# Seven block products in place of eight for the down and gate projections of a two-layer decoder trunk

## The chip, the cores and the metric

The kernel runs on one core of a Trainium2 chip. The metric is the time of one execution in device microseconds (us); each kernel is run several times and the median is given. TensorE is called PE, VectorE DVE, ScalarE ACT, GpSimd POOL, and the queue that issues most loads SP.

## What is computed

Two layers, 512 tokens, model width 1024, hidden width 4096, all in float32. Each layer is a token mixer (an mLSTM in the first, sliding-window attention in the second), and behind it come the parts that the change touches: a squared-ReLU MLP with a residual and a layer norm, and a gated per-layer input.

```python
x = layer_norm(ALPHA * x + mix, mix_ln_g[i], mix_ln_b[i])
x = layer_norm(ALPHA * x + square(relu(x @ w_up[i])) @ w_down[i], mlp_ln_g[i], mlp_ln_b[i])
x = x + sigmoid(x @ w_gate[i] + b_gate[i]) * (p[i] @ w_proj[i])
```

`w_up` is 1024x4096, `w_down` 4096x1024, `w_gate` 1024x1024, `w_proj` 256x1024.

## The kernel before

Each float32 matrix product is made of three PE matmuls (`mm3`, lines 87 to 90): every operand is split into a high part in the format fp32r and a low part that is what remains, and high*high, high*low and low*high are summed in PSUM. A split is a copy on ACT (line 76) and a subtraction on DVE, for some weights on POOL (line 77). Weights stream from memory in tiles of 128x1024 (`load_w`): the raw tile `wraw` has 3 buffers, the parts `whi` and `wlo` have 6 each, so the split for a tile waits until the tile six places before it has been used by PE.

The residual stream lives in four tiles `res` of 128 tokens x 1024. `XH` and `XL` hold the two parts of x, transposed (contraction on partitions), for all 512 tokens.

- `mlp` takes the hidden width in two halves of 2048 columns. For each, 16 up products (`wstat`, one weight tile each, 24 matmuls of 512 tokens) are squared by ACT and DVE and split into `hh` and `hl`. Then down: for each half of the 1024 output columns, four PSUM banks (one for 128 tokens each) collect 16 contraction blocks, 16*3 matmuls of 512 columns to a bank; `add_res` adds the bank to `res`. Behind the last one `ln_finish` normalises a tile of tokens and `transpose_in` puts it into `XH` and `XL`.
- `ple` takes the two halves of the output columns: for each 128 tokens first the `w_proj` product (2*3 matmuls), then the gate product (8*3 matmuls); DVE adds the bias, ACT takes the sigmoid, DVE multiplies and adds to `res`. In layer 0 it then transposes x for the next layer, scales `res` on POOL and spills it.

In what follows a line number is that of the kernel of which it is told; the changed kernel has its own. The order on each engine is set by a scheduler that the framework runs over the program, within the dependences; on the chip each engine and each DMA queue works through its own list in that order. PSUM has 5 banks for products (`mm`) and 3 for transposes (`tp`).

## Time and profile before

| what | value |
| --- | --- |
| median of 3 runs | 1259.3 us (1258.25 to 1262.23) |
| span of the profiled execution | 1256.3 us |
| median less span (what lies around the span) | 3.0 us |
| mean granted PE clock | 0.994 |
| busy PE / DVE / ACT / POOL | 1225.7 / 645.7 / 439.6 / 181.7 us |

The profile gives one execution, and for it no time but the span, so 3.0 us is the median's distance from it. A group line of the profile gives line, engine, operation, output <- inputs, shapes and count, then busy time and mean duration in ns, then the idle time of the engine just before these instructions and who ended it. A timeline line gives start and duration in us and, in brackets, the idle time before it. Durations of instructions that follow each other overlap by some tens of ns, matmuls by more, so the time that one costs is read from start to start.

### The profile page before, as it was taken

Reading aid. Unit: us, or ns where it says so; the run is one execution under the profiler, and the core shown is the slowest. Engines: PE = TensorE matmul, PEld = TensorE weight load, DVE = VectorE, ACT = ScalarE, POOL = GpSimd, SP = SyncE. Lnnn points to the kernel's source line nnn. Section 1 sums busy time; section 2 is a strip of 40 time slices with the busy share of each in tenths; the row PEclk is TensorE's granted clock in tenths of the full one; section 3 lists DMA queues with packets and bytes.
Section 4 is the critical chain, followed back from the end, with each engine's and each line's share of the span. In section 5 each row is a group of like instructions: output and inputs, shape, how many; then the busy total and the mean of one; then the engine's idle time right before and its main releaser. Section 6 shows DMA issues by size and latency. Waiting matters only on the chain.

```text
span 1256.3 us, 15515 instructions
## 1 busy us (share of the span) xinstructions
PE 1225.7 (98%) x6110; PEld 1041.3 (83%) x6110; DVE 645.7 (51%) x1061; ACT 439.6 (35%) x766; POOL 181.7 (14%) x261
## 2 busy tenths in 40 slices
PE   8999999999999999999999899999999999999998
PEld 8899987888888888888889788788888888888887
DVE  7556565744323444238555778485433244423663
ACT  4544542443212343123334555234322134421230
POOL 1011113200000000003076553530000000000100
PEclk9999999999999999999999999999999999999999
DMA  7222225333222423124233111443323332322231
GB/s 245 89 88 68 84 68 201 118 118 101 83 86 72 133 97 101 68 95 140 93 118 117 52 34 35 150 136 101 101 68 96 105 113 90 101 86 82 74 119 42
DMA packets 35704, 124.53 MB, mean 99 GB/s; under 512 B 4064, under 2 KB 4592, under 8 KB 35632
## 3 DMA queue, kind: packets, MB, share of 16 engines
q1 hardware_dynamic: 33552, 116.46, 28.1%
q0 software_dynamic: 2080, 7.09, 1.6%
q8 instruction: 48, 0.79, 0.2%
q14 instruction: 24, 0.20, 0.0%
HBM read 119.34 MB, written 4.19 MB: 98 GB/s over the span
## 4 chain that ended last, share of the span: by engine, by line
PE 86%; DVE 6%; DMA 3%; ACT 2%; issue 2%; POOL 1%; SPq 0%; ACTq 0%; DVEq 0%; POOLq 0%
PE mm L88 27%; PE mm L90 27%; PE mm L89 27%; PE tp L129 1%; DMA res<-in_x_dram 1%; DMA xraw<-in_xT_dram 1%; ACT pr L693 1%; DVE res L146 1%; DMA res<-spill 1%; PE tp L88 1%; PE tp L89 1%; PE tp L90 1%; DVE QS L662 1%; POOL rs L138 0%; DVE pr L697 0%
## 5 line engine op out<-in xcount | busy, mean ns | idle before, releaser
L76 ACT CAST whi<-wraw 128x1024 fp32r<-128x1024 f32 (+1 forms) x200 | 207.6, 1039 | 554.0 <-PE mm L90 291.2
L77 DVE TENSOR_TENSOR wlo<-wraw,whi 128x1024 fp32r<-128x1024 f32 (+1 forms) x176 | 214.7, 1223 | 357.7 <-ACT whi L76 356.8
L89 PE MATMUL mm<-XL,whi 128*128 128x512 f32 (+1 forms) x640 | 235.4, 369 | 0.0
L90 PE MATMUL mm<-XH,wlo 128*128 128x512 f32 (+1 forms) x640 | 235.3, 369 | 0.0
L88 PE MATMUL mm<-XH,whi 128*128 128x512 f32 (+1 forms) x640 | 234.3, 369 | 0.7 <-ACT ot L225 0.7
L88 PE MATMUL mm<-whi,hh 128*128 128x512 f32 x512 | 202.7, 396 | 0.0
L89 PE MATMUL mm<-wlo,hh 128*128 128x512 f32 x512 | 202.6, 396 | 0.0
L90 PE MATMUL mm<-whi,hl 128*128 128x512 f32 x512 | 202.5, 395 | 0.0
L88 PE MATMUL mm<-whi,XH 128*128 128x512 f32 (+2 forms) x424 | 146.7, 346 | 0.9 <-DVE s L554 0.5
L90 PE MATMUL mm<-whi,XL 128*128 128x512 f32 (+2 forms) x424 | 147.1, 347 | 0.0
L89 PE MATMUL mm<-wlo,XH 128*128 128x512 f32 (+2 forms) x424 | 146.5, 346 | 0.0
L88 PEld LDWEIGHTS mm<-XH,whi 128*128 128x128 f32 x640 | 120.1, 189 | 21.1 <-ACT ot L225 1.2
L90 PEld LDWEIGHTS mm<-XH,wlo 128*128 128x128 f32 x640 | 120.9, 189 | 19.9
L89 PEld LDWEIGHTS mm<-XL,whi 128*128 128x128 f32 x640 | 120.9, 189 | 19.8
L138 POOL TENSOR_TENSOR rs<-rs,nhalf 128x1 f32<-128x1 f32 x16 | 22.8, 1426 | 732.1 <-DVE rs L137 732.1
L90 PEld LDWEIGHTS mm<-whi,hl 128*128 128x128 f32 x512 | 96.5, 188 | 23.0
L88 PEld LDWEIGHTS mm<-whi,hh 128*128 128x128 f32 x512 | 96.5, 188 | 22.9
L89 PEld LDWEIGHTS mm<-wlo,hh 128*128 128x128 f32 x512 | 96.5, 188 | 22.8
L89 PEld LDWEIGHTS mm<-wlo,XH 128*128 128x128 f32 x424 | 81.7, 193 | 8.2 <-issue 1.5
L88 PEld LDWEIGHTS mm<-whi,XH 128*128 128x128 f32 x424 | 81.4, 192 | 8.0 <-DVE q L652 0.8
L90 PEld LDWEIGHTS mm<-whi,XL 128*128 128x128 f32 x424 | 81.5, 192 | 6.5 <-issue 0.8
L77 POOL TENSOR_TENSOR wlo<-wraw,whi 128x1024 fp32r<-128x1024 f32 x24 | 58.9, 2463 | 55.0 <-ACT whi L76 55.0
(246 smaller groups left out, 1476.8 us busy)
## 6 DMA issues: line engine op xcount, KB each, us to landing
wraw<-in_w_up_dram SPq DMA_DIRECT2D x64, 512.0 KB, 3.6
wraw<-in_w_down_dram SPq DMA_DIRECT2D x64, 512.0 KB, 3.5
wraw<-in_w_gate_dram SPq DMA_DIRECT2D x16, 512.0 KB, 3.5
wraw<-in_w_vo_dram SPq DMA_DIRECT2D x19, 412.0 KB, 3.2
wraw<-in_w_qk_dram SPq DMA_DIRECT2D x8, 512.0 KB, 4.5
wraw<-in_w_out_dram SPq DMA_DIRECT2D x8, 512.0 KB, 3.9
wraw<-in_w_q_dram SPq DMA_DIRECT2D x8, 512.0 KB, 3.4
wraw<-in_w_o_dram SPq DMA_DIRECT2D x8, 512.0 KB, 3.4
```

The source lines that it names most:

```text
L76: ACT.copy(hi, raw)
L77: eng.tensor_sub(lo, raw, f32(hi))
L88: PE.matmul(o, lh, rh, start=start, stop=False)
L89: PE.matmul(o, lh, rl, start=False, stop=False)
L90: PE.matmul(o, ll, rh, start=False, stop=stop)
L129: PE.transpose(pt[:, tsl(j)], src[:, tsl(b + j)], ident)
L138: GP.tensor_tensor(dst, dst, nhalf[:, :n], ALU.pow)
L146: V.scalar_tensor_tensor(res[t], res[t], rs, b, ALU.mult, ALU.add)
L662: V.tensor_sub(QS[other, hs, tsl(t)], pv[own], f32(QS)[own, hs, tsl(t)])
L693: ACT.activation(pt_[:, par, pr, :], scs[pr][:, par, :], AF.Exp, scale=ASCALE, bias=nm[:, par, pr:pr + 1], accum_out=sm[:, par, pr:pr + 1])
```

## The change

A product of two matrices in 2x2 blocks takes eight block products; the change takes seven, with sums of blocks on both sides (Winograd's form of Strassen's scheme). It is used for down and for the gate. The blocks of the activations are A11, A12 (tokens 0 to 255), A21, A22 (tokens 256 to 511), split over the contraction; those of the weights are r11, r21 (output columns 0 to 511) and r12, r22 (columns 512 to 1023). The products, in this order, with the operand on the left that is named in the code: M1 = A11 r11, M2 = A12 r21, M5 = S1 (r12-r11), M6 = S2 (r22-r12+r11), M7 = S3 (r22-r12), M3 = S4 r22, M4 = A22 (r22-r12+r11-r21). Here S1 = A21+A22, S2 = S1-A11, S3 = A11-A21, S4 = A12-S2.

- `mlp` now takes the hidden width in four quarters of 1024 columns: 8 up products, then `seven`, in which each product takes 128 tokens (a = 0, then 1) x 512 columns x 4 contraction blocks: 2*4*3 = 24 matmuls of 512 columns, two PSUM banks.
- The sums of activations are made in `evac` of the last four up products of a quarter, on POOL (four subtractions or additions of 128x256 for each), and split by ACT and DVE (`both_parts`). Tiles `S23` hold S2 and S3, `S4A` holds S4 and A22.
- The sums of weights are eight POOL subtractions of 128x1024 in each `seven`, written over the raw tiles; each result is split again, so a `seven` has 14 splits of 128x1024 where these products had 8.
- The results are summed by `on`: DVE adds banks to `res` and to a tile `T`, POOL adds `T` to `res`.
- The square now is one DVE instruction that reads the PSUM bank (line 605) and a copy of the relu by ACT; before it was two ACT instructions and a DVE product in SBUF (lines 485 to 487).
- The layer norm in front of the gate writes its sums of blocks by `put_seven` (copies by ACT, sums by DVE and POOL, seven splits for two tiles of tokens); the layer norm in front of the MLP scales `res` by ALPHA on POOL, which `add_res` did before.
- `ple` makes all eight `w_proj` products first and copies them to SBUF; `p` lies in a part of `XH`, `XL` that the gate no longer reads. The gate's `on` has DVE and POOL steps like that of `mlp`.
- The raw weights of `seven` lie in six buffers `rb` and two of `wraw`; broadcast biases have 2 buffers where there were 4.

The core of the diff (`ple` has the same pattern with its own `on`):

```diff
-    def ln_finish(t, st, g, b, xh=True):
+    def ln_finish(t, st, g, b, put=None):
         mv = small.tile([P, 2], F32, tag="mv", name="mv")
         V.bn_aggr(mv, st)
         rs = small.tile([P, 1], F32, tag="rs", name="rs")
         rsqrt_eps(rs, mv[:, 1:2], 1)
         V.scalar_tensor_tensor(res[t], res[t], mv[:, 0:1], g, ALU.subtract, ALU.mult)
         V.scalar_tensor_tensor(res[t], res[t], rs, b, ALU.mult, ALU.add)
-        transpose_in(res[t], t, XH, XL)
+        if put is None:
+            transpose_in(res[t], t, XH, XL)
+            GP.tensor_scalar(res[t], res[t], ALPHA, 0.0, ALU.mult, ALU.add)
+        else:
+            put(t)
...
+    def seven(A_, wsrc, on):
+
+        w0, w1 = wsrc(0), wsrc(1)
+        r11, r21 = two((w0, 0, True)), two((w0, 2, False))
+        r12, r22 = two((w1, 0, True)), two((w1, 2, True))
+
+        def ops(raw):
+            out = []
+            for c in range(2):
+                hi = wpool.tile([P, 1024], F32R, tag="whi", name="whi", bufs=6)
+                lo = wpool.tile([P, 1024], F32R, tag="wlo", name="wlo", bufs=6)
+                split(raw[c], 1024, hi, lo)
+                out.append((hi, lo))
+            return out
+
+        def product(name, w, step):
+            banks = [mm_bank(), mm_bank()]
+            for a in range(2):
+                for k in range(4):
+                    h, l = A_[name](k, a)
+                    wh, wl = w[k // 2]
+                    sl = slice((k % 2) * 512, (k % 2 + 1) * 512)
+                    mm3(banks[a], h, l, wh[:, sl], wl[:, sl], k == 0, k == 3)
+                on(step, a, banks[a])
+
+        product("A11", ops(r11), "M1")
+        product("A12", ops(r21), "M2")
+        for c in range(2):
+            GP.tensor_sub(r11[c], r12[c], r11[c])
+        product("S1", ops(r11), "M5")
+        for c in range(2):
+            GP.tensor_sub(r12[c], r22[c], r12[c])
+            GP.tensor_sub(r11[c], r22[c], r11[c])
+        product("S2", ops(r11), "M6")
+        product("S3", ops(r12), "M7")
+        product("S4", ops(r22), "M3")
+        for c in range(2):
+            GP.tensor_sub(r21[c], r11[c], r21[c])
+        product("A22", ops(r21), "M4")
...
+    def both_parts(dst, src, eng=V):
+
+        ACT.copy(dst[0], src)
+        eng.tensor_sub(dst[1], src, f32(dst[0]))
...
+    def put_seven(t):
+
+        a = t % 2
+        raws = []
+        for b in range(2):
+            pt = tp_bank()
+            for j in range(4):
+                PE.transpose(pt[:, tsl(j)], res[t][:, tsl(4 * b + j)], ident)
+            raw = xr()
+            ACT.copy(raw, pt)
+            raws.append(raw)
+            if t < 2:
+                v = raw.rearrange("p (k c) -> p k c", c=P)
+                both_parts((XH[:, 4 * b:4 * b + 4, tsl(t)], XL[:, 4 * b:4 * b + 4, tsl(t)]), v)
+        if t < 2:
+            half0[t] = raws
+            return
+        a11, a12 = half0[a]
+        a21, a22 = raws
+        s1 = xr()
+        V.tensor_add(s1, a21, a22)
+        GP.tensor_sub(a21, a11, a21)
+        V.tensor_sub(a11, s1, a11)
+        V.tensor_sub(a12, a12, a11)
+        sl = tsl(a)
+        kc = lambda x: x.rearrange("p (k c) -> p k c", c=P)
+        both_parts([x[:, :, sl] for x in sp["S1"]], kc(s1))
+        both_parts([x[:, 0, :, sl] for x in sp["S23"]], kc(a11))
+        both_parts([x[:, 1, :, sl] for x in sp["S23"]], kc(a21))
+        both_parts([x[:, 0, :, sl] for x in sp["S4A"]], kc(a12))
+        both_parts([x[:, 1, :, sl] for x in sp["S4A"]], kc(a22))
...
             def evac(ps, j, a, b):
-                r = pm.tile([P, S], F32, tag="relu", name="relu", bufs=3)
-                ACT.activation(r[:, a:b], ps[:, a:b], AF.Relu)
-                ACT.activation(hh[j // 2][:, j % 2, a:b], r[:, a:b], AF.Square)
-                V.tensor_mul(r[:, a:b], r[:, a:b], r[:, a:b])
-                V.tensor_sub(hl[j // 2][:, j % 2, a:b], r[:, a:b], f32(hh[j // 2])[:, j % 2, a:b])
-            nj = 2 * NPAIR
+                if j >= 4 or a == 0:
+                    h = xr()
+                    if j < 4:
+                        h0[j] = h
+                else:
+                    h = h0[j]
+                ACT.activation(h[:, a:b], ps[:, a:b], AF.Relu)
+                V.scalar_tensor_tensor(h[:, a:b], ps[:, a:b], 0.0, h[:, a:b], ALU.max, ALU.mult)
+                k = j % 4
+                if j < 4:
+                    if a == 0:
+                        both_parts([x[:, k, :] for x in A11], h[:, :256])
+                    return
+                g = h0[k]
+                both_parts([x[:, k, :] for x in A12], h[:, :256])
+                s1 = pm.tile([P, 256], F32, tag="s1", name="s1", bufs=2)
+                GP.tensor_add(s1, g[:, 256:], h[:, 256:])
+                GP.tensor_sub(g[:, 256:], g[:, :256], g[:, 256:])
+                GP.tensor_sub(g[:, :256], s1, g[:, :256])
+                GP.tensor_sub(h[:, :256], h[:, :256], g[:, :256])
+                both_parts([x[:, k, :] for x in sp["S1"]], s1)
+                two_ = lambda x: x.rearrange("p (b c) -> p b c", c=256)
+                both_parts([x[:, :, k, :] for x in sp["S23"]], two_(g))
+                both_parts([x[:, :, k, :] for x in sp["S4A"]], two_(h))
...
+                lo_, hi_ = slice(0, 512), slice(512, 1024)
+                r0, r1 = res[a], res[2 + a]
+                if step == "M1":
+                    ACT.copy(T[:, a, :], bank)
+                    GP.tensor_add(r0[:, lo_], r0[:, lo_], T[:, a, :])
+                elif step == "M2":
+                    V.tensor_add(r0[:, lo_], r0[:, lo_], bank)
+                    if last:
+                        V.bn_stats(sts[a][:, 0, :], r0[:, lo_])
+                elif step == "M5":
+                    V.tensor_add(r1[:, hi_], r1[:, hi_], bank)
+                    V.tensor_add(r0[:, hi_], r0[:, hi_], bank)
+                elif step == "M6":
+                    V.tensor_add(T[:, a, :], T[:, a, :], bank)
+                    GP.tensor_add(r0[:, hi_], r0[:, hi_], T[:, a, :])
+                elif step == "M7":
+                    V.tensor_add(T[:, a, :], T[:, a, :], bank)
+                    GP.tensor_add(r1[:, hi_], r1[:, hi_], T[:, a, :])
+                    GP.tensor_add(r1[:, lo_], r1[:, lo_], T[:, a, :])
+                    if last:
+                        V.bn_stats(sts[2 + a][:, 1, :], r1[:, hi_])
+                elif step == "M3":
+                    V.tensor_add(r0[:, hi_], r0[:, hi_], bank)
+                    if last:
+                        V.bn_stats(sts[a][:, 1, :], r0[:, hi_])
+                        ln_finish(a, sts[a], g_, b_, put_seven)
+                elif step == "M4":
+                    V.tensor_sub(r1[:, lo_], r1[:, lo_], bank)
+                    if last:
+                        V.bn_stats(sts[2 + a][:, 0, :], r1[:, lo_])
+                        ln_finish(2 + a, sts[2 + a], g_, b_, put_seven)
+
+            at = lambda pair: lambda k, a: tuple(p[:, k, tsl(a)] for p in pair)
+            seven(sset((at(A11), at(A12))), lambda half: [A["w_down"][i, half, 4 * q + c] for c in range(4)], on)
```

Three places of the order. The first is POOL's list in a quarter. Before, from the last layer norm ahead of the MLP of layer 0 to the first ones behind it, this is all that POOL has:

```order
L138 TENSOR_TENSOR rs_2090<-rs_2090,nhalf_71 128x1
L121 DMA bc_4578<-in_ple_b_gate_dram 128x1024
L121 DMA bc_4580<-in_b_b_o_dram 128x1024
L138 TENSOR_TENSOR rs_4351<-rs_4351,nhalf_71 128x1
L138 TENSOR_TENSOR rs_4398<-rs_4398,nhalf_71 128x1
L138 TENSOR_TENSOR rs_4445<-rs_4445,nhalf_71 128x1
```

After, this stands there in the third quarter of layer 0, from the first sum for the third contraction block to the sum that S2 of the last one needs (`rb` and `wraw` are raw weights, `xr` the activations, `s1` is S1); right ahead of it stands the first of the line 520 subtractions:

```order
L614 TENSOR_TENSOR s1_3763<-xr_3592,xr_3758 128x256
L525 TENSOR_TENSOR wraw_3825<-rb_3821,wraw_3825 128x1024
L615 TENSOR_TENSOR xr_3592<-xr_3592 128x256
L520 TENSOR_TENSOR rb_3823<-rb_3835,rb_3823 128x1024
L614 TENSOR_TENSOR s1_3810<-xr_3628,xr_3805 128x256
L616 TENSOR_TENSOR xr_3592<-s1_3763,xr_3592 128x256
L646 TENSOR_TENSOR res0_1745<-res0_1745,T_2129 128x512
L525 TENSOR_TENSOR wraw_3827<-rb_3823,wraw_3827 128x1024
L646 TENSOR_TENSOR res1_1746<-res1_1746,T_2129 128x512
L615 TENSOR_TENSOR xr_3628<-xr_3628 128x256
L617 TENSOR_TENSOR xr_3758<-xr_3758,xr_3592 128x256
L616 TENSOR_TENSOR xr_3628<-s1_3810,xr_3628 128x256
```

Between the sums of activations (lines 614 to 617) stand subtractions of weights (lines 520 and 525) and two additions to `res` (line 646), which wait for M1.

The second is DVE's list at the same place, the end of the up products and the first block products. Before, in the first half of the MLP of layer 0, behind the last up product:

```order
L77 TENSOR_TENSOR wlo_2969<-wraw_2967,whi_2968 128x1024
L77 TENSOR_TENSOR wlo_2975<-wraw_2973,whi_2974 128x1024
L77 TENSOR_TENSOR wlo_3085<-wraw_3083,whi_3084 128x1024
L77 TENSOR_TENSOR wlo_3091<-wraw_3089,whi_3090 128x1024
L154 SCALAR_TENSOR_TENSOR res0_1745<-res0_1745,mm_2831 128x512
L154 SCALAR_TENSOR_TENSOR res1_1746<-res1_1746,mm_2832 128x512
L154 SCALAR_TENSOR_TENSOR res2_1747<-res2_1747,mm_2833 128x512
L77 TENSOR_TENSOR wlo_3097<-wraw_3095,whi_3096 128x1024
L77 TENSOR_TENSOR wlo_3103<-wraw_3101,whi_3102 128x1024
```

After, in the third quarter (line 77 splits weights, line 543 activations, lines 648 to 653 add banks to `res`):

```order
L77 TENSOR_TENSOR wlo_3956<-rb_3821,whi_3955 128x1024
L77 TENSOR_TENSOR wlo_3960<-rb_3823,whi_3959 128x1024
L543 TENSOR_TENSOR S1l_2124<-s1_3810,S1h_2123 128x256
L543 TENSOR_TENSOR S23l_2126<-xr_3592,S23h_2125 128x2x256
L648 TENSOR_TENSOR res0_1745<-res0_1745,mm_3883 128x512
L77 TENSOR_TENSOR wlo_3994<-rb_3829,whi_3993 128x1024
L77 TENSOR_TENSOR wlo_3998<-rb_3831,whi_3997 128x1024
L648 TENSOR_TENSOR res1_1746<-res1_1746,mm_3884 128x512
L652 TENSOR_TENSOR res2_1747<-res2_1747,mm_3921 128x512
L653 TENSOR_TENSOR res0_1745<-res0_1745,mm_3921 128x512
L543 TENSOR_TENSOR S4Al_2128<-xr_3758,S4Ah_2127 128x2x256
L543 TENSOR_TENSOR S23l_2126<-xr_3628,S23h_2125 128x2x256
```

The last row is the low part of S2 and S3 of the last contraction block, which M6 reads; ahead of it stand four splits of weights, for M6 and M7, and the additions for M2 and M5.

The third is DVE's list where the MLP of layer 0 ends and the gate begins. Before (layer norm of the second tile of tokens, up to the splits of the first for `XL`):

```order
L152 TENSOR_TENSOR res1_1746<-res1_1746,mm_4176 128x512
L519 BN_STATS lst_2120<-res1_1746 128x6
L142 BN_AGGR mv_4396<-lst_2120 128x2
L137 TENSOR_SCALAR rs_4398<-mv_4396 128x1
L145 SCALAR_TENSOR_TENSOR res1_1746<-res1_1746,mv_4396,bc_3919 128x1024
L146 SCALAR_TENSOR_TENSOR res1_1746<-res1_1746,rs_4398,bc_3921 128x1024
L134 TENSOR_TENSOR XL_65<-tp_4356,XH_64 128x4x128
L134 TENSOR_TENSOR XL_65<-tp_4363,XH_64 128x4x128
```

After, at the layer norm's end (lines 145 and 146 are the layer norm's two large steps):

```order
L145 SCALAR_TENSOR_TENSOR res2_1747<-res2_1747,mv_4777,bc_4443 128x1024
L146 SCALAR_TENSOR_TENSOR res1_1746<-res1_1746,rs_4728,bc_4445 128x1024
L77 TENSOR_TENSOR wlo_5060<-rb_4959,whi_5059 128x1024
L137 TENSOR_SCALAR rs_4779<-mv_4777 128x1
L145 SCALAR_TENSOR_TENSOR res3_1748<-res3_1748,mv_4827,bc_4443 128x1024
L137 TENSOR_SCALAR rs_4829<-mv_4827 128x1
L77 TENSOR_TENSOR wlo_5064<-rb_4961,whi_5063 128x1024
L146 SCALAR_TENSOR_TENSOR res2_1747<-res2_1747,rs_4779,bc_4445 128x1024
L543 TENSOR_TENSOR XL_65<-xr_4699,XH_64 128x4x128
L543 TENSOR_TENSOR XL_65<-xr_4708,XH_64 128x4x128
L146 SCALAR_TENSOR_TENSOR res3_1748<-res3_1748,rs_4829,bc_4445 128x1024
L543 TENSOR_TENSOR XL_65<-xr_4738,XH_64 128x4x128
```

The rows of `XL` for the first tokens, which M1 of the gate reads, now stand behind the layer norm of the third tile of tokens and behind weight splits for M5 (`wlo` from `rb`).

More of the change, by code (lines that the diff above doesn't have):

```diff
@@ L541, in ple @@
                 for k in range(2):
+                    j = k * NT + t
+                    h, l = (x[:, j // 2, (j % 2) * P:(j % 2 + 1) * P] for x in spare)
                     sl = slice(k * 512, (k + 1) * 512)
[L543 to L559 removed]
@@ L560, in ple @@
-                if last:
-                    continue
-                if half == 1:
-                    transpose_in(res[t], t, XH, XL)
-                    GP.tensor_scalar(res[t], res[t], ALPHA, 0.0, ALU.mult, ALU.add)
-                    GP.tensor_add(res[t], res[t], bo)
-                    nc.sync.dma_start(spill[t], res[t])
+                    mm3(pj, h, l, wph[:, sl], wpl[:, sl], k == 0, k == 1)
+                pjs[t, half] = pp.tile([P, 512], F32, name=f"pj{t}{half}")
+                ACT.copy(pjs[t, half], pj)
@@ new lines, in ple, with done @@
+        if not last:
+            bo = bcast(A["b_b_o"])
+        def done(t):
+            if last:
+                return
+            transpose_in(res[t], t, XH, XL)
+            GP.tensor_scalar(res[t], res[t], ALPHA, 0.0, ALU.mult, ALU.add)
+            GP.tensor_add(res[t], res[t], bo)
+            nc.sync.dma_start(spill[t], res[t])
+        at = lambda b: lambda k, a: tuple(p[:, 4 * b + k, tsl(a)] for p in (XH, XL))
+        seven(sset((at(0), at(1))), lambda half: [A["w_gate"][i, half, c] for c in range(4)], on)
@@ L783, in yoco_kernel @@
     psum_pools(pctx, mm=5, tp=3)
+    c7 = seven_pools(1, "left")
     mlp(1, "left")
     ple(1, True, "left")
+    c7.close()
     pctx.close()
```

144 lines of the change are left out of this document (90 added, 54 removed).

## The prediction

> **What bounds the kernel now.** I read the page first, then the chain that ended last, then the MLP stage by stage, then single instructions of DVE and POOL where both were at work. The page and the chain:
>
> ```profile
> span 1256.3 us, 15515 instructions
> PE 1225.7 (98%) x6110; PEld 1041.3 (83%) x6110; DVE 645.7 (51%) x1061; ACT 439.6 (35%) x766; POOL 181.7 (14%) x261
> ...
> PE 86%; DVE 6%; DMA 3%; ACT 2%; issue 2%; POOL 1%; SPq 0%; ACTq 0%; DVEq 0%; POOLq 0%
> ```
>
> PE is the bound, and POOL is nearly idle. Two stages of the first MLP, an up and a down half (start and end, length, busy time of PE, PEld, DVE, ACT, POOL, granted clock, DMA share, GB/s):
>
> ```profile
> 231.00:318.00 87.00, 87.00 (x472) 75.64 (x471) 44.60 (x62) 35.08 (x55) 2.55 (x3) 1.00 0.35 111
> 318.00:405.00 87.00, 87.00 (x373) 69.97 (x372) 21.98 (x22) 15.49 (x16) 0.00 (x0) 1.00 0.24 80
> ```
>
> PE waits for nothing there, and POOL does nothing in the down half. What a matmul costs is read from starts: the down matmuls of each half (first and last start in the row), the first up matmul behind them, and 24 gate matmuls:
>
> ```profile
> L88 PE MATMUL mm<-whi,hh x128: 392/397/400, 318.4 to 407.6; 128*128 128x512 f32 x128
> ...
> 408.34 0.39 PE L88 MATMUL mm<-XH,whi 128*128 128x512 f32 x1
> ...
> L88 PE MATMUL mm<-whi,hh x128: 390/397/477, 495.4 to 586.4; 128*128 128x512 f32 x128
> ...
> 1237.86 0.39 PE L88 MATMUL mm<-whi,XH 128*128 128x512 f32 x1
> ...
> 1243.08 0.40 PE L90 MATMUL mm<-whi,XL 128*128 128x512 f32 x1
> ```
>
> Down: 408.34-318.4 = 89.9 us for 384, 0.234 each. Up: 495.4-408.34 = 87.1 for 384, 0.227. Gate: 5.22 us for 23 steps, 0.227.
>
> **What is removed.** A down quarter had 192 matmuls of 512 columns and has 7*24 = 168; there are 8 quarters: 192 fewer, 192*0.234 = 44.9 us. Each gate has 168 where 192 stood: 48*0.227 = 10.9. Together **-55.8 us**, if PE never waits. The weights are loaded once as before. On SP the raw tiles of a quarter, six of which wait for DVE's splits, now stand ahead of all but the first of the next up tiles;
>
> ```profile
> wraw<-in_w_up_dram SPq DMA_DIRECT2D x64, 512.0 KB, 3.6
> ```
>
> an up tile lands in 3.6 us and is used for 5.4, with DMA engines busy for 0.24 to 0.35: nothing, or 3.6 us a quarter if the first came late. ACT gets 6 more splits a quarter and about as many copies as it loses; with 35 us busy in 87 it has room: nothing.
>
> **What is added, and what covers it.** The rows that price it:
>
> ```profile
> L77 POOL TENSOR_TENSOR wlo<-wraw,whi 128x1024 fp32r<-128x1024 f32 x24 | 58.9, 2463 | 55.0 <-ACT whi L76 55.0
> L607 POOL TENSOR_TENSOR ta<-q,cos 128x64 f32<-128x64 f32 x16 | 5.2, 324 | 25.2 <-DVE q L652 25.2
> L76 ACT CAST whi<-wraw 128x1024 fp32r<-128x1024 f32 x184 | 193.4, 1053 | 545.8 <-PE mm L90 289.1 <-PE mm L89 195.1 <-DMA wraw<-in_w_down_dram 14.2
> ...
> 583.75 1.22 DVE L77 TENSOR_TENSOR wlo<-wraw,whi 128x1024 fp32r<-128x1024 f32 x1
> 584.88 1.28 DVE L146 SCALAR_TENSOR_TENSOR res<-res,rs,bc 128x1024 f32<-128x1024 f32 x1
> 586.08 1.22 DVE L77 TENSOR_TENSOR wlo<-wraw,whi 128x1024 fp32r<-128x1024 f32 x1
> 587.22 1.28 DVE L134 TENSOR_TENSOR XL<-tp,XH 128x512 fp32r<-128x512 f32 x2
> ...
> 659.40 0.41 DVE L639 TENSOR_TENSOR vpl<-kv,vph 128x256 fp32r<-128x256 f32 x1
> 659.73 0.68 DVE L624 TENSOR_TENSOR kv<-mm,kvb 128x512 f32<-128x512 f32 x1
> ```
>
> From start to start DVE takes 1.14 us for a split of 1024, 1.20 for a layer norm step, 0.60 for 512, 0.33 for 256. POOL takes 2.40 us for 1024 (the mean of 2463 ns less the waits below); by the line through 64 and 1024 an estimate of 1.29 for 512 and 0.73 for 256. The ACT row shows what splits wait for: PE's release of the `whi` buffers.
>
> Busy time alone would fit. What decides is the next set: DVE and POOL at the same moments (start, duration).
>
> ```profile
> 218.67 1.28 DVE L146 SCALAR_TENSOR_TENSOR res<-res,rs,bc 128x1024 f32<-128x1024 f32 x1 [0.45 <-POOL rs L138]
> 224.02 2.79 DVE L146 SCALAR_TENSOR_TENSOR res<-res,rs,bc 128x1024 f32<-128x1024 f32 x1
> 647.84 0.68 DVE L556 TENSOR_TENSOR s<-s,mm 128x512 f32<-128x512 f32 x1
> 655.97 2.42 DVE L608 TENSOR_TENSOR tb<-kv,sin 128x64 f32<-128x64 f32 x1
> 662.09 0.21 DVE L608 TENSOR_TENSOR tb<-kv,sin 128x64 f32<-128x64 f32 x1
> ...
> 219.25 2.98 POOL L77 TENSOR_TENSOR wlo<-wraw,whi 128x1024 fp32r<-128x1024 f32 x1 [0.61 <-ACT whi L76]
> 222.69 3.03 POOL L77 TENSOR_TENSOR wlo<-wraw,whi 128x1024 fp32r<-128x1024 f32 x1
> 642.21 7.58 POOL L77 TENSOR_TENSOR wlo<-wraw,whi 128x1024 fp32r<-128x1024 f32 x3
> 655.92 2.39 POOL L77 TENSOR_TENSOR wlo<-wraw,whi 128x1024 fp32r<-128x1024 f32 x1
> ```
>
> The 64-column product of two SBUF tiles takes 0.21 us alone and 2.42 when POOL has begun a 2.39 us instruction: it ends with POOL's. L146 at 224.02 waits until POOL ends at 225.72, and POOL at 219.25 until DVE ends at 219.9. But L556, which reads one input from PSUM, keeps its 0.68 us inside three POOL instructions. So DVE instructions with two SBUF inputs and POOL's run one at a time, whole instructions. Their times add up on one resource, which I call the port. Before, POOL did nothing in the MLP.
>
> **A quarter.** On the port: POOL 8*2.40 (weight sums) + 8*1.29 (additions to `res`) + 16*0.73 (activation sums) = 41.2; DVE 22 splits of 1024 *1.14 + 12 of 256 *0.33 + 8 of 512 *0.60 = 33.9. Sum 75.1 us, against PE's 192*0.227 + 168*0.234 = 82.9. It fits on average; in one stretch it does not. Let 0 be the end of the last up product; a block product takes 5.6 us. M6 starts at 3*5.6 = 16.9 and needs the low part of S2 of its fourth block at 19.4. On the other side, the line 520 subtraction writes over a raw tile that M5's split reads; this split needs the `whi` buffer of the seventh up product, free at -5.4, and takes ACT 1.05 and DVE 1.14, so that POOL can begin at -3.2. Between these two, in the queues' order: POOL 4 of 1024, 2 of 512 (behind M1), 8 of 256: 9.6+2.6+5.8 = 18.0; DVE 5 weight splits (one for M5, two each for M6 and M7), 5 of 512, 4 of 256: 5.7+3.0+1.3 = 10.0. That makes 28.0, ending at 24.8: PE waits 5.4 us. If the three of them that belong to the second block (1.9 us) are done before -3.2, it is 3.5; with 0.1 us for each of 13 hand-overs, and 1.4 that M2 waits for the last A12 split behind a weight subtraction, 8.1. I take 5.4, since DVE's splits for M1 and M2 and POOL's eight activation sums ahead fill the port until then. M1's additions on POOL and M2's on DVE stand in the same queues; the banks they free are needed only 4*2.8 us later: nothing. But line 648 on DVE waits for POOL's first addition (line 646), and behind it stand M7's weight splits and the S2 split: this is in the 28.0.
>
> What a wait does to the clock (first row: PE's start and idle time; then windows as above):
>
> ```profile
> 226.95 1.92 PE L129 MATMUL tp<-ident,res 128*128 128x128 f32 x8 [2.44 <-DVE res L146]
> ...
> 227.00:228.00 1.00, 1.00 (x5) 1.00 (x6) 1.00 (x3) 0.00 (x0) 0.00 (x0) 0.50 0.74 250
> 229.00:230.00 1.00, 1.00 (x7) 1.00 (x7) 1.00 (x3) 0.50 (x1) 0.00 (x0) 0.50 0.00 0
> 230.00:231.00 1.00, 1.00 (x9) 1.00 (x9) 1.00 (x2) 0.00 (x0) 0.00 (x0) 0.80 0.71 254
> ...
> 835.98 1.16 PE L129 MATMUL tp<-ident,res 128*128 128x128 f32 x8 [2.64 <-DVE res L146]
> ```
>
> Behind 2.44 us of idle time the granted clock was 0.50 for over 3 us: 3*0.5+0.2 = 1.7 us lost. Behind 2.64 us the same eight transposes took 1.16 us and not 1.92: nothing lost. A wait of 5.4 us is longer than both, so 1.7; the bound below is 0. A quarter then waits 7.1 us (0 to 9.8, below), eight quarters **+56.8**.
>
> [...]
>
> **A gate.** Before, PE had no gap at the layer norm: tiles were normalised while down went on. Now M5 to M4 need tokens 256 to 511, which come from M4 of the MLP. Let 0 be the end of that product. The `w_proj` products cover 10.9 us, M1, M2, M5 16.3, M6 up to the second 128 tokens' last block 5.2: needed at 32.4. The port's work begins with M1's split, when M3 frees a buffer at -7 and ACT has copied: -6. It is, up to the last S2 split: POOL 8 weight sums and 3 of 512, 23.1; DVE 10 weight splits, 8 layer norm steps, 21 of 512: 11.4+9.6+12.6 = 33.6. Sum 56.7, ending at 50.7, **18.3 us late**. If DVE is behind from the last quarter's end, where six POOL additions and four weight splits stand ahead, M1's split comes some 5 us later and hand-overs add up to 3: 26; below, 16 if two weight sums slip behind. I take 23, nearer the backlog, since the quarter's own sum leaves one. The queued broadcast loads on POOL wait for lines 145 and 146 of the last tile; what they hold up is in this range. With one spell of half clock 24.7, two gates **+49.4**.
>
> **Smaller terms.** The end of the kernel now, last bank to last addition:
>
> ```profile
> 1251.10 0.28 PE L90 MATMUL mm<-whi,XL 128*128 128x256 f32 x1
> 1252.78 0.42 DVE L557 TENSOR_TENSOR res<-res,s 128x256 f32<-128x256 f32 x1
> ```
>
> Four steps on 256 columns become four on 512: +1; DVE is behind by some steps of M3: +2, bounds 0 and 8. Scaling `res` on POOL behind the two mixers' layer norms is four instructions each, while L146 waits for POOL there already: +1, bounds 0 and 4. The square from PSUM takes one ACT and one port instruction from each up tile; counted above.
>
> **The sum.** -55.8+56.8+49.4+3+1 = +54.4 on the span of 1256.3 gives 1310.7. The median of the runs is 3.0 us above that span, so **1314 us**.
>
> **Rivals.**
> - *The port stays off PE's path* (faster). It decides at the S2 split before M6: if the 28.0 us of port work were 22.6, the wait would be zero. For it: the average fits, and POOL's times for 256 and 512 are only estimates. If the gates' work hid too: 1259.3-55.8+4 = 1207 us. Against it: the order shown has the work in series, and the gates' 18 us are mostly rows of measured size. 0.10.
> - *Only the gates wait much.* POOL's small instructions cost 0.4 and 0.64 in place of 0.73 and 1.29 (an affine select of 512 columns is the nearest cheap one), which takes 4 us from a quarter: no wait there, 16 us in each gate: -55.8+32+3 = -21 on 1259.3, 1238; with 3.5 us in a quarter and no slow clock 1266. Around 1250. 0.13.
> - *Worse than the sum.* Waits of 8.1 with the slow clock in all quarters, 26 and two spells in the gates, 8 at the end: -55.8+78.4+58.8+12 = +93, 1353 and above if banks are held up too. 0.09.
>
> **Chances.** The forecast (1265 to 1353) has 0.68. 0.3% of this kernel is 3.8 us, about what a measurement can tell from no change. The second rival lies half below, a quarter within and a quarter above that. Faster 0.10+0.06 = 0.16; same 0.04; slower 0.80. The range 1240 to 1355 leaves out the first rival, most of the third and little else.
>
> **What would show it.** Right: PE's busy share near 90%; in each quarter a gap in PE ahead of M6's last block, released by DVE's S2 split (line 543); clock digits under 9 in the MLP; mean DVE times of lines 77 and 543 well over 1.22 and 0.69, and POOL's 1024 over 2.46; the longest gaps at both gates, first behind the `w_proj` products. Wrong: DVE's splits keep 1.2 us beside a busy POOL; quarters of 83 us, or gates without a gap. The saving itself is wrong if a block product takes other than 5.6 us.

## The result, and the profile after

The changed kernel takes 1311.1 us (median of 4 runs, 1310.0 to 1314.5) where the kernel before takes 1259.4: a ratio of 1.041, 95% interval 1.039 to 1.043. The forecast was 1314 us. The sum came out right; two of its terms did not, and they cancel, which is luck. One execution, of ten, of the kernel with both repairs (below) took 2996 us and is left out of its median.

The page of the changed kernel, the lines that answer to those of before, with the rows of busy shares and of the granted clock by slices:

```profile
span 1310.1 us, 15908 instructions
PE 1200.7 (92%) x5846; PEld 1008.3 (77%) x5846; DVE 1019.4 (78%) x1322; ACT 563.4 (43%) x977; POOL 701.3 (54%) x557
...
PE   8999999999999999986957989889999999999876
...
PEclk9999999999999999997988999999999999999979
...
PE 46%; DVE 25%; POOL 12%; issue 11%; ACT 3%; DMA 3%; SPq 0%; POOLq 0%; DVEq 0%; ACTq 0%
```

PE has 264 instructions fewer and is busy 25 us less, but the span has grown: 109 us of idle time, most of it in slices 18 to 22 (the first gate and the step into layer B) and in the last three (the second gate). The chain that ended last now runs 40% of the time through DVE, POOL and ACT.

DVE's splits (a 128x1024 took 1229 ns on average in the kernel before) by groups (busy time, mean ns of one):

```profile
L77 DVE TENSOR_TENSOR wlo<-wraw,whi 128x1024 fp32r<-128x1024 f32 x120 | 180.3, 1504 | 82.4 <-ACT whi L76 82.1
L77 DVE TENSOR_TENSOR wlo<-rb,whi 128x1024 fp32r<-128x1024 f32 x100 | 165.4, 1666 | 31.6 <-ACT whi L76 31.6
L543 DVE TENSOR_TENSOR S23l<-xr,S23h 128x512 fp32r<-128x512 f32 x40 | 47.2, 1182 | 0.0
...
L605 DVE SCALAR_TENSOR_TENSOR xr<-mm,xr 128x512 f32<-128x512 f32 x56 | 38.1, 680 | 0.0
```

The splits, with two inputs in SBUF, are stretched by a fifth to three quarters (with all sums on DVE, below, the third group's 128x512 takes 0.68 us). Line 605, which reads one input from PSUM, keeps its 0.68 us between them (0.68 there too). What PE waited for, longest sums first (us in total, times, longest):

```profile
PE tp L561 <- DVE res L146: 12.1, 4, 4.8
PE mm L88 <- DVE kv L820: 12.1, 1, 12.1
PE tp L129 <- DVE res L705: 11.4, 2, 8.7
PE mm L88 <- ACT S23h L542: 8.9, 4, 2.3
PE mm L90 <- DVE A12l L543: 7.9, 7, 1.9
PE mm L88 <- DVE res L669: 7.8, 2, 4.0
PE mm L90 <- DVE XL L543: 6.3, 2, 3.1
```

Lines 542 and 543 on S and A tiles are the quarters; lines 669, 146 and `XL` are the gates; 705 is the end of the first gate; 820 is layer B's first use of the broadcast row `kvb`, which the prediction didn't see.

By stages, from the first matmul of one to that of the next (us; the first gate ends at the first transpose of K, the second with the span; the terms of the quarters and gates are halved between the layers):

| | before | after | difference | by the prediction's terms |
|---|---|---|---|---|
| to the first gate | 587.4 | 579.1 | -8.3 | +6.5 |
| first gate | 73.3 | 124.5 | +51.2 | +19.2 |
| to the second MLP | 176.2 | 172.2 | -4.0 | +0.5 |
| second MLP | 356.9 | 348.7 | -8.2 | +6.0 |
| second gate and end | 62.5 | 85.6 | +23.1 | +22.2 |

Each MLP gained, though the prediction had it lose, and the first gate lost 32 us more than was foreseen.

### The profile page after: what moved, and what is told of

The parts are those of the page before. It is cut to its first block, busy times and chain, and to the rows that moved or that the text cites. A ratio compares the mean times of both kernels' runs of the same rounds, so it can differ in the third digit from the quotient of the medians.

```text
span 1310.1 us, 15908 instructions
## 1 busy us (share of the span) xinstructions
PE 1200.7 (92%) x5846; PEld 1008.3 (77%) x5846; DVE 1019.4 (78%) x1322; ACT 563.4 (43%) x977; POOL 701.3 (54%) x557
## 4 chain that ended last, share of the span: by engine, by line
PE 46%; DVE 25%; POOL 12%; issue 11%; ACT 3%; DMA 3%; SPq 0%; POOLq 0%; DVEq 0%; ACTq 0%
PE mm L90 14%; PE mm L88 14%; PE mm L89 14%; DVE wlo L77 6%; DVE S1l L543 2%; POOL wraw L525 2%; POOL xr L615 1%; POOL s L614 1%; DVE XL L543 1%; DVE res L705 1%; POOL res L646 1%; DVE res L146 1%; POOL xr L616 1%; DVE S23l L543 1%; DVE A12l L543 1%
## 5 line engine op out<-in xcount | busy, mean ns | idle before, releaser
L76 ACT CAST whi<-wraw 128x1024 fp32r<-128x1024 f32 (+1 forms) x160 | 164.7, 1035 | 242.1 <-PE mm L90 115.2
L77 DVE TENSOR_TENSOR wlo<-rb,whi 128x1024 fp32r<-128x1024 f32 x100 | 165.4, 1666 | 31.6 <-ACT whi L76 31.6
L88 PE MATMUL mm<-whi,XH 128*128 128x412 f32 (+2 forms) x352 | 126.4, 359 | 24.7 <-DVE kv L820 12.1
L516 POOL TENSOR_TENSOR rb<-rb 128x1024 f32<-128x1024 f32 x20 | 47.9, 2394 | 154.9 <-DVE wlo L77 153.7
L90 PE MATMUL mm<-whi,XL 128*128 128x412 f32 (+2 forms) x352 | 124.2, 355 | 6.3 <-DVE XL L543 6.3
L89 PE MATMUL mm<-wlo,XH 128*128 128x412 f32 (+2 forms) x352 | 124.9, 355 | 0.0
L76 ACT CAST whi<-rb 128x1024 fp32r<-128x1024 f32 x100 | 103.9, 1047 | 43.3 <-PE mm L89 29.3
L88 PEld LDWEIGHTS mm<-whi,XH 128*128 128x128 f32 x352 | 71.2, 202 | 32.2 <-issue 12.5
L88 PE MATMUL mm<-whi,S23h 128*128 128x512 f32 x160 | 64.4, 405 | 8.9 <-ACT S23h L542 8.9
L90 PE MATMUL mm<-whi,S23l 128*128 128x512 f32 x160 | 63.5, 408 | 1.5 <-DVE S23l L543 1.5
L520 POOL TENSOR_TENSOR rb<-rb 128x1024 f32<-128x1024 f32 x20 | 53.8, 2689 | 19.5 <-DVE rs L137 12.5
L89 PE MATMUL mm<-wlo,S23h 128*128 128x512 f32 x160 | 63.1, 404 | 0.9 <-DVE wlo L77 0.9
```

The costliest lines, as they stand in the source:

```text
L76: ACT.copy(hi, raw)
L77: eng.tensor_sub(lo, raw, f32(hi))
L88: PE.matmul(o, lh, rh, start=start, stop=False)
L89: PE.matmul(o, lh, rl, start=False, stop=False)
L90: PE.matmul(o, ll, rh, start=False, stop=stop)
L516: GP.tensor_sub(r11[c], r12[c], r11[c])
```

## The experiments

The theory was the prediction's: POOL's sums and DVE's instructions with two SBUF inputs share one port and run one at a time, so POOL's work delays the copies and splits that PE waits for. The rivals: DVE is simply short of time and needs POOL's help; or the gates' waits come from the layer norm alone. All times are medians; ratios are to runs of the kernel before on the same chip.

### The port by itself

```diff
 w = [load_w(A["w_down"][i, half, fh * 8 + kq * 4 + c], 1024) for c in range(4)]
+for hi, lo in w:
+    z = pm.tile([P, 1024], F32, tag="z", name="z", bufs=1)
+    GP.tensor_sub(z, f32(hi), f32(lo))
```

> The kernel before, and beside each of its 64 down weight tiles one POOL subtraction of 128x1024 (high less low part into a scratch tile nothing reads). No product is left out and PE's work is the same. Port theory: POOL then is busy 43% of a down half, a DVE split that meets it waits 0 to 2.4 us, half an us on average: DVE's mean for 128x1024 rises from 1.229 to 1.35 to 1.5, POOL's from 2.46 to about 2.6, and the time stays within 0.5% since DVE has 68 of 90 us to spare there. Rival, no shared port: DVE's mean stays at 1.23.

1258.6 us, ratio 0.999 (0.998 to 1.000). The splits' group in the kernel before:

```profile
L77 DVE TENSOR_TENSOR wlo<-wraw,whi 128x1024 fp32r<-128x1024 f32 x160 | 196.2, 1229 | 349.4 <-ACT whi L76 349.1
```

The same group in this kernel:

```profile
L77 DVE TENSOR_TENSOR wlo<-wraw,whi 128x1024 fp32r<-128x1024 f32 x160 | 241.9, 1520 | 270.5 <-ACT whi L76 270.2
```

Its busy times:

```profile
PE 1223.6 (97%) x6110; PEld 1038.4 (83%) x6110; DVE 739.8 (59%) x1061; ACT 438.7 (35%) x766; POOL 358.4 (29%) x325
```

One of the new instructions and DVE's beside it (start, duration):

```profile
292.25 2.79 POOL L512 TENSOR_TENSOR z<-whi,wlo 128x1024 f32<-128x1024 f32 x1 [55.31 <-DVE wlo L77]
...
292.82 2.77 DVE L488 TENSOR_TENSOR hl<-relu,hh 128x512 fp32r<-128x512 f32 x1
```

DVE has the same 1061 instructions as before and is busy 739.8 us where it was 645.7: 94 us of waiting counted as work, with 64 POOL instructions that nothing reads. Line 488, 0.69 us on average in the kernel before, takes 2.77: it ends at 295.59, 0.55 us after POOL's instruction. Time doesn't change: PE is busy 1223.6 us of a span of 1255.6 where it was 1225.7 of 1256.3. The mean of the splits, 1.52 us, lies a little above the expected 1.35 to 1.5. So a busy share of DVE beside a busy POOL is not all work, and here, where DVE had slack (busy 59% of the span), the price of the port did not show in the time.

### All sums, or the weight sums alone, on DVE

```diff
-            GP.tensor_sub(r11[c], r12[c], r11[c])
+            V.tensor_sub(r11[c], r12[c], r11[c])
```

and so for all the sums that the change brought (first run), or for the four lines of weight sums alone (second).

> The changed kernel with every sum that the seven products brought to POOL (weight sums, activation sums, additions to res, the gate's) issued on DVE in place of POOL. Port theory (DVE's two-SBUF-input instructions and POOL's run one at a time): POOL's 2.40, 1.29 and 0.73 us become 1.14, 0.60 and 0.33, so a quarter's port work falls from 75.1 to 53.1 us and DVE's own sum is 66 of 83 us. Changed kernel 1311.1; quarters lose about 3.5 of their 4.4 us excess (-28), each gate about 12 (-24), the exit of the first gate up to 8: about 1251, 1240 to 1275. DVE's mean for a split of 1024 returns to about 1.2. Rival, DVE is the short engine and POOL's help is needed: moved work adds 171 us to DVE's 1019 busy, 91% of the span, PE waits more: 1330 or above.

> Only the 80 weight sums (lines 516, 519, 520, 525) move from POOL to DVE; activation sums and additions stay on POOL. Port theory: 80*2.40 becomes 80*1.14, 10 us less on the port in each quarter and gate, where a quarter's wait was about 2.2 us with a spell of half clock: 1265 to 1285. Rival, DVE is the short engine: 91 us more on it, 1325 or above. If it equals the kernel with all sums on DVE, the small POOL instructions cost nothing.

1263.8 us, ratio 1.002 (1.001 to 1.004), and 1274.5, ratio 1.012 (1.010 to 1.014). The ranges of the two theories lie 55 and 40 us apart, and both times fall in the port's, the first 13 us above its forecast of 1251. The busy times of the version with all sums on DVE:

```profile
PE 1188.4 (94%) x5846; PEld 1006.7 (80%) x5846; DVE 989.3 (78%) x1610; ACT 564.5 (45%) x977; POOL 199.7 (16%) x269
```

One of its split groups:

```profile
L77 DVE TENSOR_TENSOR wlo<-rb,whi 128x1024 fp32r<-128x1024 f32 x100 | 121.7, 1217 | 36.5 <-ACT whi L76 36.5
```

Its second to fourth quarter (start and end, length, busy time of PE, PEld, DVE, ACT and POOL, clock, DMA):

```profile
312.46:395.38 82.92, 82.92 (x362) 67.69 (x361) 67.86 (x97) 36.95 (x52) 0.00 (x0) 1.00 0.33 102
395.38:478.29 82.91, 82.91 (x362) 67.68 (x360) 67.82 (x97) 36.96 (x52) 0.00 (x0) 1.00 0.34 102
478.29:561.20 82.91, 82.91 (x361) 67.68 (x360) 67.86 (x96) 37.78 (x53) 0.00 (x0) 1.00 0.33 102
```

The same three quarters in the changed kernel:

```profile
316.91:404.25 87.34, 84.95 (x361) 68.72 (x360) 71.22 (x67) 37.19 (x53) 55.18 (x32) 0.98 0.34 102
404.25:491.50 87.25, 84.96 (x362) 68.69 (x360) 70.32 (x65) 36.84 (x52) 55.09 (x32) 0.98 0.32 97
491.50:579.09 87.59, 85.02 (x362) 68.49 (x361) 71.55 (x67) 37.88 (x53) 53.09 (x32) 0.98 0.30 96
```

DVE was given 288 instructions more and is busy 30 us less; in a quarter it is busy 68 us where it was 71 with a third fewer instructions. PE waits for nothing in these quarters, which take the 82.9 us that the prediction worked out as PE's own. The quarters of both MLPs together are 32.0 us shorter (17.6 and 14.4, from the first block of up products to the first gate product). The weight sums are 37 of the 47 us.

The gates gained less than expected of the port: the second gate and the end take 79.1 us where they took 85.6, 6.5 less in place of 12. In the gates PE now waits for DVE itself, above all behind the layer norm:

```profile
PE tp L561 <- DVE mv L142: 18.9, 3, 9.3
```

So the quarters are freed by this move, and the gates only in part.

### The gates: the sums, or the layer norm

```diff
-        for c in range(2):
-            GP.tensor_sub(r11[c], r12[c], r11[c])
+            if sums:
+                GP.tensor_sub(r11[c], r12[c], r11[c])
```

with `sums` false in the gates; and, in the other kernel, lines 145 and 146 only where `put` is None. The first leaves out the eight weight sums of each gate, the second the two large steps of the layer norm behind each MLP.

> The changed kernel with the eight weight sums of each gate left out (M5, M6, M7 and M4 of the gates multiply with unsummed blocks); everything else as in the changed kernel. Theory A, the prediction's: the gate waits because port work up to the last S2 split ends late, and 8 POOL sums of 2.40 (19 us) of it go: most of the 15 us of waits and their slow clock in each gate go, 1311 less 25 to 36: 1275 to 1286. Theory B: the waits come ahead of the sums, from the layer norm and the splits behind it on DVE (waits behind lines 669, 146 and 543): 0 to 10 less, 1301 to 1311.

> The changed kernel with the two layer norm steps (lines 145, 146) left out behind the MLPs: the tokens go on unscaled, statistics are still taken. 8 DVE instructions of 1.2 us go from each gate, and no POOL one but what hangs on them. Theory A (port work of 56.7 us in a row): 9.6 us a gate less, 1290 to 1295. Theory B (the chain bank, layer norm, transposes, splits is what PE waits for): 9.6 us and the slow clock behind the 4.8 us wait, 11 to 15 a gate: 1281 to 1289. Under B this run gains more than the run without the gate's weight sums, under A less.

1277.9 us, ratio 1.014 (1.011 to 1.017), and 1293.2, ratio 1.025 (1.022 to 1.028). Both fall where the port's sum puts them, and the sums are worth more than the layer norm: 33 against 18 us, or 17 and 9 for a gate on average, of 19.2 and 9.6 us of work (the wait for `kvb`, 12.1 us in the changed kernel, is 9.1 and 14.1 in these two: 3 us of the first gain, and 2 us lost to the second). What PE waited for longest without the sums (line 709 here is 705 of the changed kernel, 824 is 820):

```profile
PE tp L129 <- DVE res L709: 9.1, 2, 7.3
PE mm L88 <- DVE kv L824: 9.1, 1, 9.1
```

And without the layer norm:

```profile
PE mm L88 <- DVE kv L820: 14.1, 1, 14.1
PE mm L89 <- DVE wlo L77: 12.1, 4, 5.0
```

Without the gate's sums, the waits behind lines 146 and 669 are gone from the top of the list, though the layer norm stands there unchanged. Without the layer norm, PE waits behind split weight sums (line 77), which it hardly did before. It is one queue of work: which instruction PE is found waiting for says where the queue ends, not what made it long. Theory B, to which the list of waits had led, falls.

### The row of layer B

```diff
-    nc.gpsimd.dma_start(kvb, A["kv_b"].partition_broadcast(P))
+    nc.sync.dma_start(kvb, A["kv_b"].partition_broadcast(P))
```

and so for `bq`. The rows of the changed kernel that led here, on POOL, DVE and PE:

```profile
687.55 2.34 POOL L756 TENSOR_TENSOR res<-res,bc 128x1024 f32<-128x1024 f32 x1
...
690.35 0.61 POOL L781 DMA_DIRECT2D kvb<-in_kv_b_dram  x1
...
694.86 1.29 DVE L820 TENSOR_TENSOR kv<-mm,kvb 128x512 f32<-128x512 f32 x2 [10.39 <-DMA kvb<-in_kv_b_dram]
...
695.70 0.77 PE L88 MATMUL mm<-whi,XH 128*128 128x512 f32 x1 [12.12 <-DVE kv L820]
```

> The two broadcast loads of layer B (kvb, bq) are issued by SP in place of POOL, nothing else. In the changed kernel kvb is issued at 690.35 behind POOL's last addition and memsets, and PE waits 12.1 us for it. Theory, POOL's queue holds the issue: 12 us and a spell of half clock (1.7) go, 1297 to 1300. Rival, the next wait (DVE's last splits, rotary work) takes its place: 1305 to 1311.

1298.7 us, ratio 1.031 (1.029 to 1.034): 12.4 us of the 51.7. In the kernel before POOL issued this load at 587.7, as the first gate began. The change also moves the allocation of layer B's tiles, this row with them, behind `ple`; so the load stands behind all of POOL's gate work. With both repairs (all sums on DVE, the row by SP):

> All sums on DVE and, besides, kvb and bq issued by SP. With all sums on DVE alone the time was 1263.8 and PE still waited 6.4 us for kvb. Theory: the two repairs add, -6.4 and part of a slow-clock spell: 1255 to 1258. Rival, DVE's backlog at the gate's end (7.0 us behind line 705) only moves on: 1262 to 1264.

1257.2 us, ratio 0.997 (0.995 to 1.000), as if the two repairs add; but the executions spread from 1252.8 to 1262.1, wider than the gain. The profiled one took 1262.1: the wait for `kvb` is gone from it, but later in layer B PE waits 6.1 us behind DVE's line 156, which waits for the load of the spilled `res`. Whether the faster ones have this wait isn't known. The kernel is no longer slower than the kernel before.

### Seven products in the MLPs alone

The gate of the kernel before (its `ple`) stands behind the new `mlp`; layer B's tiles stand ahead of the gate again.

```diff
-                        ln_finish(a, sts[a], g_, b_, put_seven)
+                        ln_finish(a, sts[a], g_, b_, put_plain)
```

> Seven products in the MLPs only; the gates with eight as in the kernel before (its code), key and value pools allocated ahead of the first gate as before. By stages of the two traces an MLP is 348.7 us where it was 358.6 (-9.8, waits included), and all of the loss stands in the gates and the first gate's exit (+50.9 and +24.8). Theory: the MLP alone gains what its stage shows, 1259.4-19.7+1 = 1241, 1236 to 1248. Rival, the cost at the gates comes from the MLP's hand-over (tokens 256 to 511 end last, layer norm in PE's path): it stays, 1285 to 1300.

> Seven products in the MLPs only, gates with eight, and the sums on DVE. Theory: the quarters fall from 87.3 to 82.9 us as they did with all sums on DVE in both stages, 8*4.3 = 34 us under the 1263.6 of the version with sums on POOL: 1229, 1225 to 1235. Rival, the gain in the quarters hangs on the gate's shape (layer norm split sums ahead) or DVE is late at the layer norm: 1240 to 1255.

1263.6 us, ratio 1.002 (1.001 to 1.004): neither theory. (The stages above have 8.2 us for an MLP, not the 9.8 of the expectation.) The rival has part of it: from the end of M4 to the first transpose of K this kernel takes 84.8 us where the kernel before takes 73.6 from the end of down, and from M4 of the second MLP to the end 73.7 for 62.8, 11 us more at each gate. And 1237.6 with the sums on DVE, ratio 0.982 (0.979 to 0.986): faster than both kernels, 26 us gained where 34 were expected. The quarters of the first MLP take the 82.9 us, but the two MLPs gained 15.6 and 12.5 us, not 17 each, and each gate lost 2 more. What is left to gain is the way into the gate: 87.1 us (561.8 to 648.8) for the 73.6 before. There tokens end one tile after another while down goes on; here tokens 256 to 511 all end with the last product, and DVE has the additions, the layer norm and the gate's first splits at once.

Two attempts on these 13 us. The first splits `pT` early, into the tiles of S1, gives the gate's broadcast rows tiles of their own and has SP issue `kvb` and `bq`; since the tiles of S1 must live on, layer B's tiles stand behind the gate once more. The second also puts M3 ahead of M7, does the scaling of `res` and the addition in one DVE instruction and has SP load the gate's rows. A third has the swap and the one DVE instruction without the rest.

> As the version before it, and the waits at the MLP's end attacked: pT is loaded and split behind M6 of the last quarter into the tiles of S1 (PE waited 6.25 and 6.44 us for this split, with slow clock behind), the gate's two broadcast rows get tiles of their own, kvb and bq are issued by SP. Theory: 1229 less 2*(6.3+2.5): 1208 to 1216. Rival, the wait turns into one for the layer norm of tokens 0 to 127 (DVE): 1218 to 1229.

> The version with pT split into S1's tiles (1245.5), with two edits: M3 ahead of M7, so that tokens 0 to 255 are complete one block product (5.6 us) earlier; and the scaling of res and the addition of the broadcast row as one DVE instruction in place of two on POOL, the row loaded by SP. In that version DVE held a 64-column product for 11.7 us while POOL ran back to back, and PE waited 6.8 us behind it. Theory: 6.8 and 1.7 of slow clock go, and half of the swap's 5.6 us at each gate (DVE is backlogged there): 1230 to 1235. Rival, DVE's own backlog sets the layer norm whatever the order: only the 8.5 go, 1237. Rival, the streak was not the cause: 1240 or above.

> The version with seven products in the MLPs only and sums on DVE (1237.6), with M3 ahead of M7 and the same fused instruction on DVE. PE waits 7.6 and 7.2 us in its two gates, on DVE's split of pT and layer norm. Theory, half of 5.6 us a gate: 1231 to 1234. Rival, DVE's backlog sets it: 1236 to 1239.

1245.5 us, ratio 0.988 (0.986 to 0.990); 1239.5, 0.985 (0.983 to 0.988); 1237.8, 0.984 (0.981 to 0.987). The first is slower than the version that it was to better, and outside both expectations. The wait moved from the split of `pT` to the layer norm (first row, PE), and a new one of 6.8 us stands at layer B (the other rows: DVE, POOL, PE):

```profile
572.54 2.79 PE L129 MATMUL tp<-ident,res 128*128 128x128 f32 x12 [9.44 <-DVE mv L142]
...
644.31 11.70 DVE L771 TENSOR_TENSOR ta<-kv,cos 128x64 f32<-128x64 f32 x1
...
643.23 2.40 POOL L77 TENSOR_TENSOR wlo<-wraw,whi 128x1024 fp32r<-128x1024 f32 x1
645.60 1.04 POOL L726 TENSOR_SCALAR res<-res 128x1024 f32<-128x1024 f32 x1
646.62 9.30 POOL L727 TENSOR_TENSOR res<-res,own 128x1024 f32<-128x1024 f32 x4
...
657.18 0.69 PE L795 MATMUL tp<-ident,kd 128*128 128x128 f32 x2 [6.83 <-ACT kd L792]
```

A product of 64 columns took 11.7 us (the next of this shape, line 772 at 655.93, took 0.21): POOL, whose four additions came in a row (their broadcast row had been issued on POOL's queue at 640.2, late), held the port from 643.2 to 655.9. With the four as one DVE instruction each, this wait is gone; by the ratios the kernel is 0.3% faster, some 4 us, the swap and the rows by SP included. The swap seems to have brought nothing: PE waits 9.45 us behind the layer norm, as with M7 first, and the third kernel stands where it stood without swap and fused instruction. That these 9.4 us are DVE's own backlog is argued from its gapless row there, beside a POOL that has only the layer norm's small steps; it is not shown by a run of its own.

## Why the prediction was right, and where it was not

The span grew by 53.8 us, for +54.4 forecast. The mechanism was right: PE waits for work that DVE and POOL do in turns. The nearness of the number is luck, since the quarters were put 25 us too high and the first gate 32 too low.

- **The saving, -55.8.** Right in the MLPs. A quarter without a wait takes 82.91 us for the 82.9 worked out, and with all sums on DVE the second MLP is 22.6 us shorter than before, for 22.5. The gates' 10.9 were not seen by themselves.
- **Eight quarters, +56.8.** Mechanism right, size nearly double: measured +32.0, the difference to all sums on DVE, or 4.0 for a quarter in place of 7.1. The wait of 5.4 us was mis-sized. In the second quarter of the first MLP (PE's row, with its idle time; POOL's last subtraction ahead of it, and ACT's copy of the result):

```profile
383.16 0.77 PE L88 MATMUL mm<-whi,S23h 128*128 128x512 f32 x1 [2.17 <-ACT S23h L542]
...
381.74 0.72 POOL L616 TENSOR_TENSOR xr<-s,xr 128x256 f32<-128x256 f32 x1
...
382.49 0.62 ACT L542 CAST S23h<-xr 128x512 fp32r<-128x512 f32 x1
```

  and the windows behind it, columns as above:

```profile
383.10:384.10 1.00, 0.94 (x2) 0.81 (x3) 1.00 (x2) 1.00 (x3) 0.17 (x1) 0.56 0.77 283
384.10:385.10 1.00, 1.00 (x4) 0.76 (x3) 1.00 (x2) 1.00 (x2) 0.00 (x0) 0.50 0.53 213
385.10:386.10 1.00, 1.00 (x4) 0.81 (x3) 1.00 (x3) 1.00 (x2) 0.00 (x0) 0.50 0.00 0
386.10:387.10 1.00, 1.00 (x4) 0.79 (x4) 1.00 (x3) 0.37 (x1) 0.00 (x0) 0.73 0.37 45
```

  By the prediction's clock (0 at 360.4, the start of M1) POOL and DVE take turns without a gap from -1.9, where POOL begins line 520, to 22.0, where POOL ends line 616. That is 23.9 us; the prediction had 28.0, from -3.2 to 24.8. Of the work counted there, three DVE splits of 512 and one POOL step of 256 ran ahead of this stretch or behind it. PE goes on at 22.7, once ACT has copied the block; it did not wait for DVE's low part, with which the prediction's sum ends (24.0 here). And it ran dry at 20.5, not 19.4. That POOL is merely slow would not do it: its 13 instructions in the stretch are 17.3 us at the prediction's prices, an estimate, and would end at 15.4 without the turns. The place was right in four quarters (M6, 2.2 us each); in the first and last of each MLP the wait fell on M2 instead (1.85 us, `A12l`), with 0.7 to 1.3 us at M5 or M6. The spell of half clock lost 0.44+0.50+0.50+0.27 = 1.7 us, the price used.
- **Two gates, +49.4.** The second gate and the end came out within a microsecond (+23.1 for +22.2), and the gate's sums are worth 17 us a gate, near the 19.2 of the port's sum. The form was wrong: not one wait ahead of the last S2 split, but six of 0.8 to 4.8 us from the end of the MLP on (at the first gate a seventh, 0.9), since the same queue holds the layer norm and the splits of tokens. So the size of the second gate is in part luck: PE's gaps there sum to 14.8 us where 23 were taken; slow clock, the token transposes that now stand in the gate and a longer tail make up for it. From its first matmul to its last (columns as above):

```profile
1224.51:1300.03 75.52, 60.76 (x249) 47.52 (x247) 74.28 (x76) 33.30 (x49) 41.86 (x21) 0.86 0.04 16
```

  A mean clock of 0.86 over 75.5 us, idle time included, is more than the one spell of 1.7 us that was counted; how much of it PE would have used was not taken apart. The lower bound of 16 us was also misreckoned: two weight sums of 2.40 taken off 18.3 leave 13.5.
- **What was left out.** The first gate lost 32 us more than predicted. The row `kvb` is 12.4 of them: the prediction's part on a gate said that the broadcast loads wait on POOL and put what they hold up "in this range", but did not follow what is queued behind POOL's gate work in the next stage. The rest stands at that gate's end: 8.7 and 2.6 us behind line 705, and slow clock. The longest wait behind this line stays with all sums on DVE (7.0 us) and is not there with the gate of eight products; it was not taken apart further. The stretch from there to K's first transpose in the changed kernel (clock 0.75):

```profile
656.00:703.60 47.60, 25.40 (x100) 20.60 (x101) 25.42 (x33) 9.65 (x16) 31.07 (x55) 0.75 0.34 116
```

- **The tail and ALPHA**, +4: from the end of the last matmul to the end of the span the changed kernel takes 10.1 us where it was 4.9, so the tail is +5.2 for +3, inside its bounds. ALPHA's +1 lies inside the differences of the other stages and was not tested apart.
- **The rivals.** "The port stays off PE's path" fell: the port is on it in every quarter and gate. "Only the gates wait much" was wrong on the quarters by 4.0 us each, and low on the gates; by its own sum, too, 4 us off a wait of 5.4 would have left 1.4 in a quarter. "Worse than the sum" (1353 and above) did not come.
- **The signs.** Right: PE's share (92%), the stretched splits, POOL's 1024 (2.66 us over the 80 weight sums). Half right: the gap ahead of M6's fourth block is there in four quarters of eight, and ACT's copy ends it, not DVE's split. Wrong: the clock's digits stay at 9 in the MLPs (0.98 over a quarter), the longest gap is at layer B, not at a gate, and the first gap of a gate falls among the `w_proj` products, not behind them.

What the runs show of the port: beside POOL's 2.79 us, DVE's line 488 took 2.77 us where the kernel before has 0.69; the 64-column product of 11.7 us was held through the rest of one POOL instruction and five whole ones; and moving the sums back to DVE gained 47 us.

## What to carry over

Before work is put on an idle POOL, count it, at POOL's durations, and DVE's instructions with two SBUF inputs as one queue, and compare with the deadline of the stretch, not with the average: here the average fitted (75 of 83 us) and each quarter still lost 4 us. Where DVE does the same sum in half the time (line 516: 1.21 us on average with all sums on DVE, 2.39 on POOL), give it to DVE even if its busy share looks high, since part of that share may be waiting. And when a change moves an allocation, follow the loads that move with it into the next stage's queue: one 256 KB row cost a quarter of the whole loss.

## What was not expected of the hardware

A wait of 2.17 us was followed by 3.5 us at about half clock; one of 2.25 us, at the same product in the second MLP, was not (the changed kernel, PE's row):

```profile
1032.11 0.50 PE L88 MATMUL mm<-whi,S23h 128*128 128x512 f32 x1 [2.25 <-ACT S23h L542]
```

The windows behind this wait, clock in the third column from the end:

```profile
1032.11:1033.11 1.00, 1.00 (x4) 0.86 (x5) 1.00 (x2) 1.00 (x2) 0.10 (x1) 1.00 0.55 213
1033.11:1034.11 1.00, 1.00 (x6) 0.79 (x5) 1.00 (x2) 1.00 (x2) 0.00 (x0) 1.00 0.63 246
```

So the same wait costs 2.2 or 3.9 us, and the quarters show it: 87.3 us with the spell, 85.5 without (0.4 of this difference is no spell: with all sums on DVE the same quarters take 82.9 and 82.6 us). And a blocked DVE instruction did not get its turn behind the POOL instruction that blocked it: the 64-column product, 11.7 us for 0.21, ended 0.09 us after the last of six.
